# A two-layer decoder trunk (block-sparse attention, then gated DeltaNet): elementwise work moved from GpSimd to VectorE and ScalarE, and the order of all work planned anew

## The chip, the cores and the metric

The kernel runs on one core of a Trainium2 chip, in one launch. The metric is the device time of that launch in microseconds (us); the time before is 693.81 us, the median of three runs (692.59 to 696.28). A core has TensorE (PE; PEld is its weight load), VectorE (DVE), ScalarE (ACT), GpSimd (POOL) and SyncE (SP, which here only issues DMAs). Each works through its own list of instructions in order.

## The reference, cut to what matters

The input is x, 512 positions of 1024 values in float32, and a condition c. Two layers follow, each with weights of some 16 MB for its input projection:

```
for i in range(2):
    mod = silu(c) @ ada_w[i] + ada_b[i];  shift, scale, gate = split(mod, 3)
    h = x * (1 + scale) + shift
    y = moba_branch(h) if i == 0 else gdn_branch(h)
    x = layer_norm(sqrt(2) * x + gate * y)

moba_branch: q, k, v, z = split(h @ w_in)        # 8 heads of 128
    o = softmax over own 256-block (causal) and selected past blocks
    return (o * silu(z)) @ w_out
gdn_branch:  q, k, v, z, a, b = split(h @ w_in)
    q, k, v = silu(causal conv of 4 taps);  q, k L2-normalised
    g = -exp(a_log) * softplus(a + dt_bias);  beta = sigmoid(b)
    per head, chunks: solve (I + tril(beta * k k^T * decay)) for u, w,
    then the recurrence over chunks, RMS norm, times silu(z), @ w_out
```

## The kernel before, in words

All large products are float32 work done in three passes on a shorter format: each operand is split into a high half (ScalarE copies it, `wh`, `hH`, `oH`) and a low half (the rest, `wl`, `hL`, `oL`, a subtraction), and TensorE adds high x high, low x high and high x low (`mm3`). So each of the weight pieces that are read (`raw`, 512 KB each, two buffers, `fetch` at L254) has four subtractions of 512 columns per group of 256 weight columns behind it (`cut`, L268): the first of each half-piece on VectorE, the second on GpSimd. A raw buffer is free again when its last subtraction is done.

Stages. (1) Front: for each of eight column blocks j, `first_mod` computes the modulation from 1 MB of `aw` on VectorE (`accj`, some six multiply-adds of 256 columns), `first_h` makes block j of h (`hH`, `hL`), `first_w` splits a 768-column weight block (`wrh` on ScalarE, `wrl` on GpSimd except for j = 0), and `first_mm` multiplies into `z_ps`. (2) Layer 0: the other projections, attention (`att`, scores `s_ps`, probabilities `pr`, small statistics `nm`), and beside it the remaining modulations (`mods`, tile `acc`, from `ga`). The output projection (`out0`, `y_ps`) reads `wl_0o`, `wh_0o`; before these are cut, `cut` multiplies the raw weights by the layer's gate on GpSimd (`gate=0`). (3) Switch: `evac` adds the product to xn, `norm0` normalises, `mod_t` transposes to `h_ps` and makes the next `hH`, `hL`; `prep` loads small tensors (`crow`, `wab`, `dtb`) and transposes `crow` (`crow_t`); `residual` multiplies xn by `g0r` and adds `b0r` on GpSimd; `decays` computes the log decays (`spl`, `g_`, `gc`) in some 30 dependent small steps. (4) Layer 1: projections `gq`, `gk`, `gv`, `z`, convolutions (`conv`, `pre`), and for each of four pairs of heads `inverse` (triangular factor `L`, its block diagonal `Lc` through DRAM to `Lr`, 15 steps on `u`, then small 32-wide products `X_ps`, `U_ps`), `values` (transposes `vt_ps`), `recur`, `gated` (`ogn`, `og_ps`) and the output products `y_ps`. The other banks' results of layer 1 go through ScalarE (`et`) and are added on GpSimd (`evac1`). (5) Tail: `finish` normalises four row tiles (`fin`) and stores them.

What sets the order. The program is written by a planner at build time (`Weave`, L34 to L138): every piece of work is a generator that yields an engine and an assumed cost; the planner takes the piece that could start first, and among equals the one with the smaller number in `RANK` (L179). So all instruction lists, SP's DMAs too, are fixed by these numbers and costs. Engines marked DVE2 and POOL exclude one another in the planner's account. Line 148 is the helper through which every instruction is recorded, so in the profile all rows have that line and one goes by tiles.

Of the kernel before, what the change touches and what calls it, by code (L numbers as in the profile page):

```python
# [19 lines left out]
H = 8  # L20
# [10 lines left out]
def flat(ap, dims, offset=0):  # L31
    return bass.AP(tensor=ap.tensor, offset=ap.offset + offset, ap=dims)


class Weave:
# [78 lines left out]

    def run(self, *until):
        while True:
            self._settle()
            if all(u in self.marks for u in until):
                return
            best, first = None, None  # L120
            for p in self.pieces:
                if p[3][0] in ("slot", "wait"):
                    continue
                start = self._start(p[3][0], p[3][2])
                if best is None or start < first - 1e-6:
# [9 lines left out]
            self._go(best, first + cost + self.LAT.get(engine, 0.0))  # L135
# [29 lines left out]

@with_exitstack
def trunk(ctx: ExitStack, tc: tile.TileContext, x, c, ada_w, ada_b, ln_g, ln_b, moba_w_in, moba_w_out,
# [11 lines left out]
    RANK = dict(fetch=16, kv0=26, qk0=82, kv00=105, cols2=77, mods=48, loads=9, evac0=82, conv0=93, decays=4, evac1=82, zs=11, conv=65, prep=68, resid=21, decay_f=38, inverse=0, inner=102, queries=5, values=94, recur=87, gated=42, keep0=47, norm0=18, mod_t=85, cut0=63, cut1=78)  # L179
# [59 lines left out]
    for name, n in (("mm", 0), ("s", 0), ("t", 1), ("o", 0), ("raw", 2), ("wp", 2), ("wx", 2), ("aw", 3), ("wr", 3),  # L239
# [3 lines left out]
        pl.slots(name, n)  # L243
# [24 lines left out]
    def cut(g0, g1):  # L268
# [3 lines left out]
        for name, w, c0, slot, width, r0, nk, gate in groups[g0:g1]:  # L272
# [8 lines left out]
            for h in range(2):  # L281
                t = yield "wait", ("raw", name, h)
                t = max(t, t0)
                raw = raws.pop((name, h))
                if gate is not None:
                    t = max(t, (yield "wait", ("gate", gate)))
                    hk = nk // 2
                    r3 = raw.rearrange("p (k n) -> p k n", n=width)
                    t = yield "POOL", pool(1024), t
                    ge.tensor_mul(r3, r3, gates[gate][:, None, c0:c0 + width].to_broadcast([P, hk, width]))  # L290
                ends = []
                for q in range(2):
                    sl = slice(q * 512, q * 512 + 512)
                    r = raw[:, sl]
                    if wide == width:
                        d = slice(1024 * h + q * 512, 1024 * h + q * 512 + 512)
                        dh, dl = wh[:, d], wl[:, d]
                    else:
                        r = r.rearrange("p (k n) -> p k n", n=width)
                        d = slice(4 * h + 2 * q, 4 * h + 2 * q + 2)  # L300
                        dh, dl = wh3[:, d, 0:width], wl3[:, d, 0:width]
                    e = yield "ACT", act(512), t
                    se.activation(dh, r, AF.Copy)
                    eng = "POOL" if q and gate is None else "DVE"
                    e = yield (eng if eng == "POOL" else "DVE2"), (pool if eng == "POOL" else dve)(512), e
# [149 lines left out]
    def first_w(j):  # L455
# [12 lines left out]
        e = yield ("POOL", pool(768), e) if j else ("DVE2", dve(768), e)  # L468
        (ge if j else ve).tensor_sub(wl, wr, wh.bitcast(F32))
# [127 lines left out]
    def att(hd, i):  # L597
# [22 lines left out]
        else:  # L620
# [198 lines left out]
    def mod_t(hf, k2):  # L819
# [87 lines left out]
    def prep():  # L907
# [32 lines left out]

        yield "POOL", 0.8, 0.0
        low = l1.tile([P, 32], F32, name="low")
        ge.memset(low, 0.0)
        ge.memset(low[:, 0:16], 1.0)
        for g in range(4):
            lg = low[32 * g:32 * g + 32]
            ge.affine_select(lg, lg, pattern=[[0, 32]], compare_op=ALU.is_ge, fill=0.0, base=-16,
                             channel_multiplier=1)
# [9 lines left out]
        masks.update(blk=blk, low=low, blk32=blk32, id32=id32, d16=d16)  # L958
        pl.mark("masks", e)

    def residual():
# [6 lines left out]
        t = yield "wait", "out0", ("gate_row", 1)  # L968
# [8 lines left out]
        for st in range(ST):  # L977
            e = yield "wait", ("hT", st // 2, 0), ("hT", st // 2, 1), ("hT", st // 2, 2), ("hT", st // 2, 3)
            e = max(e, eg)
            for q in range(2):  # L980
                qs = slice(q * 512, q * 512 + 512)
                e = yield "POOL", pool(512), e
                ge.tensor_mul(xn[:, st, qs], xn[:, st, qs], g0r[:, qs])
                e = yield "POOL", pool(512), e
                ge.tensor_add(xn[:, st, qs], xn[:, st, qs], b0r[:, qs])
# [166 lines left out]
    def proj1():  # L1152
# [34 lines left out]
        for sp_ in order1[2:]:  # L1187
            s, p = sp_[0], int(sp_[1])
            dep = yield "wait", ("w", "1" + sp_)
            if s == "o":  # L1190
                for p_, st in last if p == H // 2 - 2 else [] if p == H // 2 - 1 else [(p, st) for st in range(ST)]:
# [4 lines left out]
                    for q in pq:  # L1196
                        if q == p_:
                            dep = max(dep, (yield "wait", ("ogT", p_, st)))
                        for g2 in range(2):
# [7 lines left out]
                            if q == p_:  # L1207
                                pl.add(RANK["evac1"], evac1(os_[g2], st, g2, f"y{p_}", e))
# [76 lines left out]
    def inverse(p):  # L1285
# [36 lines left out]
        for h in range(2):  # L1322
# [12 lines left out]
        fac[p, "L"] = L
        pl.mark(("L", p), e1)

        e = yield "POOL", pool(1024), e1
        Lm = f4(p, "Lm", tag="UT")
        ge.tensor_mul(v8(Lm), v8(L), masks["blk"][:, None, :].to_broadcast([P, 8, P]))  # L1340
        e = yield "DVE", 1.87, e
        Lc = f4(p, "Lc", [P, 8, 16])
        ve.reduce_sum(Lc, v8(Lm).rearrange("p t (b j) -> p t j b", j=16), axis=AX.X)
# [31 lines left out]
        e = yield "wait", ("Lb", p), ("aq", p)  # L1375
        Lb = fac[p, "Lb"]
# [3 lines left out]
        L8, U8 = v8(L), v8(Uf)  # L1380
# [3 lines left out]
        g32 = [slice(32 * g, 32 * g + 32) for g in range(4)]  # L1384
# [80 lines left out]

    def inner(p):

        e = yield "wait", ("L", p)
        Lb = fac[p, "Lb"] = f4(p, "Lb", [P, 8, 32])

        e += 2.5
        for g in range(4):
            pp = slice(32 * g, 32 * g + 32)
            e1 = yield "POOL", pool(256), e
            ge.tensor_mul(Lb[pp], v8(fac[p, "L"])[pp, :, pp], masks["low"][pp, None, :].to_broadcast([32, 8, 32]))
        pl.mark(("Lb", p), e1)
# [198 lines left out]
    def finish(st):  # L1675
# [26 lines left out]
        def normed(qs, e1, nb):  # L1702
# [4 lines left out]
            e1 = yield "POOL", pool(512), e1  # L1707
            ge.tensor_add(f[:, qs], f[:, qs], fin["b"][:, qs])
# [59 lines left out]
```

## Time and profile before

| | before |
|---|---|
| median of three runs | 693.81 us |
| profiled execution | 695.99 us, its span 694.3 us |
| busy: PE, DVE, ACT, POOL | 628.1, 507.6, 310.2, 246.1 us |
| mean granted clock of TensorE | 0.963 |
| read from HBM | 78.82 MB |

In the views a row of a timeline says: start, duration, engine, line, operation, tiles out<-in, shapes, count, and in brackets how long the engine was idle before it and what released it. Several equal instructions in a row are merged, the duration is then that of all. The last 0.08 us or so of a VectorE instruction overlap with the next one, so that two of 0.68 us take 1.28 us. PEclk is the clock that TensorE was granted: 1.00 is 2.4 GHz, 0.50 is 1.2 GHz.

### The profile page before, as it was taken

The page shows a single profiled execution, that of the slowest core. Times are in us where ns is not written, and L with a number is a line of the kernel's source. Part 1 is how long each engine was busy: PE and PEld are TensorE (multiplying, and loading weights), DVE is VectorE, ACT ScalarE, POOL GpSimd, SP SyncE. Part 2 cuts the span into 40 slices and gives each one's busy share as a digit, 9 for nine tenths or more (in the row PEclk, how much of TensorE's full clock was granted, in tenths as well). Part 3 has the DMA queues.
Part 4 walks back from the last instruction along what each step waited for, and adds up shares of the span by engine and source line. Part 5 has one row for each costly group of instructions (what it writes and reads, how often), then busy time and mean ns, then how long its engine had stood idle before and what let it go on. Part 6 is the DMA issues. An engine that isn't in the chain of part 4 may idle for free. (4 is left out here: it accounts for less than half of the span.)

```text
span 694.3 us, 12082 instructions
## 1 busy us (share of the span) xinstructions
PE 628.1 (90%) x4488; PEld 539.7 (78%) x4488; DVE 507.6 (73%) x1155; ACT 310.2 (45%) x822; POOL 246.1 (35%) x203
## 2 busy tenths in 40 slices
PE   8699999999999999599978979999999978999991
PEld 7588788977988778599866857788887757997871
DVE  5875888687685777367677678587737798688687
ACT  2334555543531334114334763765375457633451
POOL 0235122402214042305862352252226332744625
PEclk8899999999999999899999999999989989999997
DMA  9992645747545331504114353424133204412203
GB/s 262 298 290 78 187 137 176 242 143 224 152 156 168 102 122 62 159 2 122 31 34 90 92 141 85 117 58 133 33 91 84 77 2 117 135 59 64 92 2 121
DMA packets 83022, 82.25 MB, mean 118 GB/s; under 512 B 8762, under 2 KB 71443, under 8 KB 82451
## 3 DMA queue, kind: packets, MB, share of 16 engines
q1 hardware_dynamic: 82882, 81.45, 40.6%
q8 instruction: 35, 0.57, 0.3%
q14 instruction: 25, 0.20, 0.1%
q10 hardware_dynamic: 80, 0.03, 0.0%
HBM read 78.82 MB, written 2.65 MB: 117 GB/s over the span
## 5 line engine op out<-in xcount | busy, mean ns | idle before, releaser
L148 DVE SCALAR_TENSOR_TENSOR acc<-ga,cs,acc 128x512 f32<-128x512 f32 x56 | 51.1, 924 | 19.1 <-DMA ga<-in_ada_w_dram 19.0
L148 POOL TENSOR_TENSOR raw_0o<-raw_0o,gate 128x1024 f32<-128x1024 f32 x8 | 19.1, 2388 | 58.2 <-DMA raw_0o<-in_moba_w_out_dram 40.4
L148 ACT ACTIVATE pr<-s_ps,nm 128x256 f32<-128x256 f32 (+1 forms) x48 | 20.7, 436 | 41.0 <-DVE nm L148 35.6
L148 PE MATMUL z_ps<-wh_1z,hH 128*128 128x256 f32 (+1 forms) x128 | 37.8, 295 | 0.0
L148 PE MATMUL y_ps<-wh_0o,oH 128*128 128x256 f32 x128 | 37.7, 294 | 0.0
L148 PE MATMUL y_ps<-wh_0o,oL 128*128 128x256 f32 x128 | 37.0, 289 | 0.0
L148 PE MATMUL y_ps<-wl_0o,oH 128*128 128x256 f32 x128 | 37.0, 289 | 0.0
L148 PE MATMUL z_ps<-wh_1z,hL 128*128 128x256 f32 (+1 forms) x128 | 36.4, 285 | 0.0
L148 PE MATMUL z_ps<-wl_1z,hH 128*128 128x256 f32 (+1 forms) x128 | 36.4, 284 | 0.0
L148 PE MATMUL gk_ps<-hH,wl_1k 128*128 128x512 f32 x64 | 26.5, 415 | 3.6 <-DVE wl_1k L148 3.6
L148 POOL TENSOR_TENSOR wrl<-wr,wrh 128x768 fp32r<-128x768 f32 x7 | 14.0, 2002 | 44.6 <-ACT wrh L148 44.6
L148 PE MATMUL gq_ps<-hH,wh_1q 128*128 128x512 f32 (+1 forms) x80 | 29.5, 368 | 0.0
L148 PE MATMUL v_ps<-wh_0v,hH 128*128 128x256 f32 x96 | 28.3, 295 | 0.0
L148 PE MATMUL gq_ps<-hL,wh_1q 128*128 128x512 f32 (+1 forms) x80 | 27.9, 349 | 0.0
L148 PE MATMUL gk_ps<-hH,wh_1k 128*128 128x512 f32 x64 | 27.9, 435 | 0.0
L148 PE MATMUL gq_ps<-hH,wl_1q 128*128 128x512 f32 (+1 forms) x80 | 27.8, 348 | 0.0
L148 PE MATMUL gv_ps<-hH,wh_1v 128*128 128x512 f32 x64 | 27.8, 434 | 0.0
L148 PE MATMUL y_ps<-wh_1o,ogh 128*128 128x512 f32 x64 | 27.7, 432 | 0.0
L148 PE MATMUL z_ps<-hH,wh_0z 128*128 128x512 f32 x64 | 26.6, 416 | 1.0 <-ACT qT L148 1.0
L148 PE MATMUL v_ps<-wl_0v,hH 128*128 128x256 f32 x96 | 27.1, 283 | 0.0
L148 PE MATMUL v_ps<-wh_0v,hL 128*128 128x256 f32 x96 | 27.1, 283 | 0.0
L148 DVE SCALAR_TENSOR_TENSOR accj<-aw,cs,accj 128x256 f32<-128x256 f32 x45 | 26.4, 653 | 0.8 <-DMA aw<-in_ada_w_dram 0.8
(335 smaller groups left out, 2234.6 us busy)
## 6 DMA issues: line engine op xcount, KB each, us to landing
ga<-in_ada_w_dram SPq DMA_DIRECT2D x64, 256.0 KB
aw<-in_ada_w_dram SPq DMA_DIRECT2D x14, 512.0 KB
raw_0z<-in_moba_w_in_dram SPq DMA_DIRECT2D x8, 512.0 KB
raw_0o<-in_moba_w_out_dram SPq DMA_DIRECT2D x8, 512.0 KB
raw_1z<-in_gdn_w_in_dram SPq DMA_DIRECT2D x8, 512.0 KB
raw_1q<-in_gdn_w_in_dram SPq DMA_DIRECT2D x8, 512.0 KB
raw_1k<-in_gdn_w_in_dram SPq DMA_DIRECT2D x8, 512.0 KB
raw_1v<-in_gdn_w_in_dram SPq DMA_DIRECT2D x8, 512.0 KB
```

The source lines that it names most:

```text
L148: r = f(*args, **kwargs)
```

## The change

The planner can now leave an elementwise operation to either VectorE or GpSimd (`either`, `_choose`); it takes the one that would end first, with 49/20 = 2.45 us added for GpSimd. Of the operations that are offered so, all but two come out on VectorE. GpSimd's list shrinks from 183 rows to 60; what is left are the powers (`rstd`, `rk`, `rq`, `rms`), masks, memsets and two copies of `T64` per pair. Further: layer 0's gate no longer multiplies the weights but the product, in PSUM, on VectorE (12 tiles of 512 columns); the softmax's probabilities are scaled on ScalarE, and the small statistics that added or compared two tiles use a per-partition operand instead; `L` is made by four ScalarE scalings and one VectorE product for each head; `Lc` and `Lb` are taken with 32 small ScalarE and 16 VectorE instructions for the four pairs in place of GpSimd's masked products and VectorE's reduction; layer 1's results are all added by VectorE from PSUM (`evac1` is gone); z2 and z3 are projected earlier. All numbers in `RANK` are new. Cut to its core:

```diff
-    RANK = dict(fetch=16, ..., prep=68, resid=21, ..., mod_t=85, cut0=63, cut1=78)
+RANK = dict(pool=49, fetch=22, ..., prep=8, resid=0, ..., mod_t=58, cut0=75, cut1=78)
...
+    def _choose(self, engine, cost, dep):
+        if "/" not in engine:
+            return engine, cost, self._start(engine, dep)
+        ends = []
+        for n, c in zip(engine.split("/"), cost):
+            t = self._start(n, dep)
+            ends.append((t + c + (RANK["pool"] / 20 if n == "POOL" else 0.0), n, c, t))
+        return min(ends)[1:]
+def either(n, ptr=0):
+    return "DVE2/POOL", (dve(n, ptr), pool(n))
...
 cut
-                    t = yield "POOL", pool(1024), t
-                    ge.tensor_mul(r3, r3, gates[gate][...])
+                    t, g = yield *either(1024), t
+                    eng_(g).tensor_mul(r3, r3, gates[gate][...])
-                    eng = "POOL" if q and gate is None else "DVE"
-                    (ge if eng == "POOL" else ve).tensor_sub(dl, r, dh.bitcast(F32))
+                    e, g = yield *either(512), e
+                    eng_(g).tensor_sub(dl, r, dh.bitcast(F32))
...
-        want(f"0o{g}", moba_w_out[0], g * GW, "wx" if g < 2 else "wp", gate=0)
-    order1 = "z0 q0 k0 q1 v0 v1 k1 v2 q2 k2 z1 k3 q3 v3 o0 z2 z3 o1 o2 o3".split()
+        want(f"0o{g}", moba_w_out[0], g * GW, "wx" if g < 2 else "wp")
+    order1 = "z0 q0 k0 q1 v0 v1 k1 v2 q2 k2 z1 k3 q3 z2 v3 z3 o0 o1 o2 o3".split()
...
 first_w (mod_t, residual and finish alike)
-        (ge if j else ve).tensor_sub(wl, wr, wh.bitcast(F32))
+        e, g = yield *either(768), e
+        eng_(g).tensor_sub(wl, wr, wh.bitcast(F32))
...
 att
-            ve.tensor_max(m, m, nb)
+            ve.tensor_scalar(m, m, nb, None, op0=ALU.max)
-        ve.tensor_scalar_mul(pr[:, :n], pr[:, :n], rv)
+        se.activation(pr[:, :n], pr[:, :n], AF.Copy, scale=rv)
...
 evac
+        if first_ is not None:
+            e = max(e, (yield "wait", ("gate", 0)))
+            e = yield "DVE", dve(512), e
+            ve.tensor_mul(o, o, gates[0][:, gs])
...
 inverse
-                ve.scalar_tensor_tensor(L[:, h, t], gk[:, t], bk2[...], F[:, h, t], op0=ALU.mult, op1=ALU.mult)
+                se.activation(L[:, h, t], F[:, h, t], AF.Copy, scale=bk2[...])
+            ve.tensor_mul(L[:, h], gk, L[:, h])
-        ge.tensor_mul(v8(Lm), v8(L), masks["blk"][...])
-        ve.reduce_sum(Lc, v8(Lm).rearrange("p t (b j) -> p t j b", j=16), axis=AX.X)
+        for g in g32:
+            se.activation(Lc[g], L8[g, :, g.start:g.start + 16], AF.Copy, scale=half[0][g])
+        for g in g32:
+            ve.scalar_tensor_tensor(Lc[g], L8[g, :, g.start + 16:g.stop], half[1][g], Lc[g], ...)
```

Three places in the instruction lists. The first is SP's list of DMAs at the switch from layer 0 to layer 1, before:

```order
L148 DMA raw_0o_2661<-in_moba_w_out_dram 128x4x256
L148 DMA raw_0o_2763<-in_moba_w_out_dram 128x4x256
L148 DMA g0r<-in_ln_g_dram 128x1024
L148 DMA b0r<-in_ln_b_dram 128x1024
L148 DMA raw_0o_2860<-in_moba_w_out_dram 128x4x256
L148 DMA crow<-in_gdn_conv_w_dram 96x128
L148 DMA wab<-in_gdn_w_in_dram 128x8x16
L148 DMA dtb<-in_gdn_dt_bias_dram 128x8
L148 DMA dtb<-in_gdn_a_log_dram 128x8
L148 DMA raw_1z_2879<-in_gdn_w_in_dram 128x4x256
```

and after the change:

```order
L164 DMA raw_0o_2643<-in_moba_w_out_dram 128x4x256
L164 DMA raw_0o_2665<-in_moba_w_out_dram 128x4x256
L164 DMA raw_1z_2784<-in_gdn_w_in_dram 128x4x256
L164 DMA raw_1z_2805<-in_gdn_w_in_dram 128x4x256
L164 DMA g0r<-in_ln_g_dram 128x1024
L164 DMA b0r<-in_ln_b_dram 128x1024
L164 DMA crow<-in_gdn_conv_w_dram 96x128
L164 DMA wab<-in_gdn_w_in_dram 128x8x16
L164 DMA dtb<-in_gdn_dt_bias_dram 128x8
```

Here `raw_0o` are the weight pieces of layer 0's output projection, `raw_1z` the first of layer 1. The last `raw_0o` stood behind `g0r` and `b0r`, which need memory of the attention stage; now all `raw_0o` and the first `raw_1z` stand ahead of them.

The second is VectorE's list in the front, block j = 1 to j = 2, before:

```order
L148 SCALAR_TENSOR_TENSOR accj<-aw,cs,accj 128x256 x6
L148 TENSOR_TENSOR accj<-accj 128x256
L148 TENSOR_TENSOR hL<-ht,hH 128x512
L148 TENSOR_TENSOR ab_268<-mod_ps,colb 128x2
L148 TENSOR_SCALAR accj<-aw,cs 128x256 x2
L148 SCALAR_TENSOR_TENSOR accj<-aw,cs,accj 128x256 x6
L148 TENSOR_TENSOR accj<-accj 128x256
```

and after:

```order
L164 SCALAR_TENSOR_TENSOR accj<-aw,cs,accj 128x256 x6
L164 TENSOR_TENSOR accj<-accj 128x256
L164 TENSOR_TENSOR hL<-ht,hH 128x512
L164 TENSOR_TENSOR wrl<-wr,wrh 128x768
L164 TENSOR_TENSOR ab_273<-mod_ps,colb 128x2
L164 TENSOR_SCALAR accj<-aw,cs 128x256 x2
L164 SCALAR_TENSOR_TENSOR accj<-aw,cs,accj 128x256 x6
L164 TENSOR_TENSOR accj<-accj 128x256
```

One `wrl` subtraction of 768 columns per block has come into the list, behind the `hL` of the same block.

The third is TensorE's list in layer 1 where the values of the first pair of heads are transposed (`vt_ps`), before:

```order
L148 MATMUL gv_ps_1_3974<-hH,wh_1v_3763 128x512
L148 MATMUL gv_ps_1_3974<-hH,wl_1v_3764 128x512
L148 MATMUL gv_ps_1_3974<-hL,wh_1v_3763 128x512
L148 MATMUL vt_ps_0_4070<-ident,vc_4039 128x128 x4
L148 MATMUL gv_ps_0_4069<-hH,wh_1v_3887 128x512
L148 MATMUL gv_ps_0_4069<-hH,wl_1v_3888 128x512
L148 MATMUL gv_ps_0_4069<-hL,wh_1v_3887 128x512
L148 MATMUL vt_ps_1_4087<-ident,vc_4058 128x128 x4
L148 MATMUL gv_ps_0_4069<-hH,wh_1v_3887 128x512
```

and after:

```order
L164 MATMUL gv_ps_0_4060<-hH,wh_1v_3887 128x512
L164 MATMUL gv_ps_0_4060<-hH,wl_1v_3888 128x512
L164 MATMUL gv_ps_0_4060<-hL,wh_1v_3887 128x512
L164 MATMUL vt_ps_0_4108<-ident,vc_4042 128x128 x4
L164 MATMUL gv_ps_1_4105<-hH,wh_1v_3887 128x512
L164 MATMUL gv_ps_1_4105<-hH,wl_1v_3888 128x512
L164 MATMUL gv_ps_1_4105<-hL,wh_1v_3887 128x512
```

The transposes of `vt_ps_0` stood right behind the projection `gv_ps_1` of their own pair; now the 24 matmuls of the next pair's `gv_ps_0` stand between them, and nine more before `vt_ps_1`.

## Rows read from the trace of the kernel before

**Rows 1.** Page, parts 1 and 2: busy time of each engine; TensorE in 40 slices.

```profile
PE 628.1 (90%) x4488; PEld 539.7 (78%) x4488; DVE 507.6 (73%) x1155; ACT 310.2 (45%) x822; POOL 246.1 (35%) x203
...
PEclk8899999999999999899999999999989989999997
```

**Rows 2.** Waits of TensorE: for what; us in total, times, longest us.

```profile
PE crow_t L148 <- DMA wab<-in_gdn_w_in_dram: 7.5, 1, 7.5
PE mod_ps L148 <- DVE accj L148: 6.3, 3, 3.1
PE vt_ps L148 <- DVE vc L148: 4.5, 2, 3.8
PE gk_ps L148 <- DVE wl_1k L148: 3.6, 1, 3.6
...
PE pt_ps L148 <- DVE nm L148: 1.9, 2, 1.7
PE gate_ps L148 <- DVE mod L148: 1.7, 1, 1.7
PE h_ps L148 <- ACT ht L148: 1.6, 1, 1.6
```

**Rows 3.** Timeline at the switch: SP.

```profile
280.28 0.42 SPq L148 DMA_DIRECT2D raw_0o<-in_moba_w_out_dram  x1
280.75 0.50 SPq L148 DMA_DIRECT2D crow<-in_gdn_conv_w_dram  x1
```

**Rows 4.** The same stretch: GpSimd.

```profile
256.64 2.36 POOL L148 TENSOR_TENSOR raw_0o<-raw_0o,gate 128x1024 f32<-128x1024 f32 x1 [0.55 <-DMA raw_0o<-in_moba_w_out_dram]
...
287.05 2.36 POOL L148 TENSOR_TENSOR raw_0o<-raw_0o,gate 128x1024 f32<-128x1024 f32 x1 [9.81 <-DMA dtb<-in_gdn_dt_bias_dram]
```

**Rows 5.** The same stretch: TensorE.

```profile
287.35 0.39 PE L148 MATMUL crow_t<-ident,crow 96*128 96x96 f32 x1 [7.47 <-DMA wab<-in_gdn_w_in_dram]
```

**Rows 6.** The same stretch: VectorE.

```profile
248.63 1.28 DVE L148 TENSOR_TENSOR wl_0o<-raw_0o,wh_0o 128x512 fp32r<-128x512 f32 x2
...
256.66 2.36 DVE L148 TENSOR_TENSOR mod<-mod,colb 128x8 f32<-128x8 f32 x1
...
290.10 1.40 DVE L148 TENSOR_TENSOR wl_0o<-raw_0o,wh_0o 128x512 fp32r<-128x512 f32 x2 [9.31 <-ACT wh_0o L148]
```

**Rows 7.** Windows: us, busy by engine (count), PEclk, DMA share, GB/s.

```profile
35.00:40.00 5.00, 5.00 (x30) 4.31 (x29) 0.98 (x4) 1.53 (x2) 1.85 (x1) 0.93 1.15 305
...
285.00:290.00 5.00, 2.65 (x13) 2.68 (x14) 0.00 (x0) 0.56 (x2) 2.88 (x4) 0.50 0.62 162
...
295.00:300.00 5.00, 5.00 (x44) 5.00 (x44) 2.38 (x4) 0.00 (x0) 0.00 (x0) 1.00 0.01 3
...
290.00:680.00 390.00, 361.84 (x2949) 311.83 (x2948) 287.96 (x642) 194.94 (x560) 165.41 (x146) 0.97 0.28 76
680.00:694.00 14.00, 0.31 (x2) 0.00 (x0) 10.88 (x14) 1.52 (x2) 7.20 (x6) 0.65 0.35 134
```

**Rows 8.** Timeline, front, j = 1 to 4.

```profile
18.92 4.01 DVE L148 SCALAR_TENSOR_TENSOR accj<-aw,cs,accj 128x256 f32<-128x256 f32 x6
...
19.74 2.12 POOL L148 TENSOR_TENSOR wrl<-wr,wrh 128x768 fp32r<-128x768 f32 x1 [18.38 <-ACT wrh L148]
...
30.89 2.46 DVE L148 SCALAR_TENSOR_TENSOR accj<-aw,cs,accj 128x256 f32<-128x256 f32 x6
```

**Rows 9.** Groups by tile and shape: busy us, mean ns, idle before, releaser.

```profile
L148 DVE TENSOR_REDUCE Lc<-Lm 128x128 f32<-128x1024 f32 x4 | 7.8, 1939 | 1.3 <-POOL Lm L148 1.3
...
L148 DVE TENSOR_TENSOR xn<-xn,y_ps 128x512 f32<-128x512 f32 x23 | 15.7, 682 | 9.4 <-PE y_ps L148 9.0
```

**Rows 10.** Timeline in layer 1, first pair of heads: TensorE.

```profile
406.41 0.63 PE L148 MATMUL vt_ps<-ident,vc 128*128 128x128 f32 x4 [3.79 <-DVE vc L148]
```

**Rows 11.** Timeline of the tail: VectorE.

```profile
686.22 1.75 DVE L148 SCALAR_TENSOR_TENSOR fin<-xn,lnmv,g1r 128x512 f32<-128x512 f32 x1
```

**Rows 12.** Timeline of the tail: GpSimd.

```profile
684.41 4.68 POOL L148 TENSOR_TENSOR fin<-fin,b1r 128x512 f32<-128x512 f32 x3
```

More of the change, by code (lines that the diff above doesn't have):

```diff
@@ L32, in flat @@
     return bass.AP(tensor=ap.tensor, offset=ap.offset + offset, ap=dims)
+RANK = dict(pool=49, fetch=22, kv0=50, qk0=45, kv00=40, cols2=20, mods=50, loads=25, evac0=96, conv0=17, decays=11, evac1=60, zs=49, conv=45, prep=8, resid=0, decay_f=67, inverse=4, inner=0, queries=40, values=94, recur=96, gated=7, keep0=43, norm0=37, mod_t=58, cut0=75, cut1=78)
 class Weave:
@@ L119, in run @@
                 return
-            best, first = None, None
+            best, first, choice = None, None, None
             for p in self.pieces:
@@ L134, in run @@
             self.busy[engine] = first + cost
-            self._go(best, first + cost + self.LAT.get(engine, 0.0))
+            end = first + cost + self.LAT.get(engine, 0.0)
+            self.ran = engine, first, cost
+            self._go(best, (end, engine) if either else end)
 class InOrder:
@@ L177, in trunk, with eng_ @@
     DLAT = 2.0
-    RANK = dict(fetch=16, kv0=26, qk0=82, kv00=105, cols2=77, mods=48, loads=9, evac0=82, conv0=93, decays=4, evac1=82, zs=11, conv=65, prep=68, resid=21, decay_f=38, inverse=0, inner=102, queries=5, values=94, recur=87, gated=42, keep0=47, norm0=18, mod_t=85, cut0=63, cut1=78)
+    def eng_(name):
+        return ge if name == "POOL" else ve
     def dma(kb, dep=0.0):
@@ L939, in prep @@
                          channel_multiplier=-1)
[L941 to L948, printed above, removed]
         e = yield "DVE", 0.6, pl.busy["POOL"] + 0.2
@@ L967, in residual @@
         eg = e + DLAT
-        t = yield "wait", "out0", ("gate_row", 1)
+        t = yield "wait", "out0", ("gate_row", 1), *(("ya", st, q) for st in (2, 3) for q in range(2))
         e = yield dma(512, t)
@@ L981, in residual @@
                 qs = slice(q * 512, q * 512 + 512)
[L982 to L985, printed above, removed]
+                e, g = yield *either(512), e
+                eng_(g).tensor_mul(xn[:, st, qs], xn[:, st, qs], g0r[:, qs])
+                e, g = yield *either(512), e
+                eng_(g).tensor_add(xn[:, st, qs], xn[:, st, qs], b0r[:, qs])
         pl.mark("x1", e)
@@ L1327, in inverse @@
                 te.matmul(gk[:, t], kc[h][:, ts(t)], kc[h][:, ts(t)], start=True, stop=True)
-            e1 = max(e, e1, (yield "wait", ("F", p)), lev)
+            e2 = max(e, (yield "wait", ("F", p)), lev)
             F = fac[p, "F"]
             for t in range(ST):
-                e1 = yield "DVE", dve(128, 1), e1 - 0.2
-                ve.scalar_tensor_tensor(L[:, h, t], gk[:, t], bk2[:, t, h:h + 1], F[:, h, t], op0=ALU.mult,
-                                        op1=ALU.mult)
+                e2 = yield "ACT", act(128, 1), e2 - 0.2 * (t > 0)
+                se.activation(L[:, h, t], F[:, h, t], AF.Copy, scale=bk2[:, t, h:h + 1])
+            e1 = yield "DVE", dve(512), max(e1, e2)
+            ve.tensor_mul(L[:, h], gk, L[:, h])
             pl.give("s", e1)
[L1335 to L1341, printed above, removed]
-        Lc = f4(p, "Lc", [P, 8, 16])
-        ve.reduce_sum(Lc, v8(Lm).rearrange("p t (b j) -> p t j b", j=16), axis=AX.X)
+        Lc = f4(p, "Lc", [P, 8, 16])
+        Lb = f4(p, "Lb", [P, 8, 32])
+        yield "POOL", 0.3, 0.0
+        ge.memset(Lb, 0.0)
+        L8 = v8(L)
+        g32 = [slice(32 * g, 32 * g + 32) for g in range(4)]
+        half = [masks["blk32"][:, 0:1], masks["blk32"][:, 16:17]]
+        e2 = e1
+        for g in g32:
+            e2 = yield "ACT", act(128, 1), e2 - 0.2
+            se.activation(Lc[g], L8[g, :, g.start:g.start + 16], AF.Copy, scale=half[0][g])
+        e = e1 + 0.4
+        for g in g32:
+            e = yield "DVE2", dve(128, 1), e - 0.1
+            ve.scalar_tensor_tensor(Lc[g], L8[g, :, g.start + 16:g.stop], half[1][g], Lc[g], op0=ALU.mult, op1=ALU.add)
+        e = max(e, e2 + 0.4)
+        for g in g32:
+            e2 = yield "ACT", act(128, 1), e2 - 0.2
+            se.activation(Lb[g, :, 0:16], L8[g, :, g.start:g.start + 16], AF.Copy, scale=half[1][g])
         e = yield dma(128, e)
@@ L1379, in inverse @@
         fac[p, "Uf"] = Uf
[L1380 removed]
+        U8 = v8(Uf)
         yield "POOL", 1.1, 0.0
@@ L1464, in inverse @@
         pl.mark(("inv", p), e)
[L1466 to L1476, printed above, removed]
     def queries(p):
```

58 lines of the change are left out of this document (19 added, 39 removed), and 1 row of the table rcol.

## The prediction, made before the changed kernel was run

> **What bounds the kernel now.** I read the page first. TensorE is busy for 628.1 us of a span of 694.3, VectorE for 507.6 and GpSimd for 246.1 [rows 1]. TensorE executes the same set of matmuls before and after the change, in another order. So the change can win at most what TensorE loses: 66 us of idle time, 14 of them in the tail behind the last matmuls [rows 7], and what the stretches with a lower clock cost. The view of TensorE's waits, read next, says for whom it waits. The reader is to see there that the largest sum is one single wait of 7.5 us for `crow_t`, put down to a DMA (`wab`), and that most others end on VectorE: `mod_ps` 6.3, `vt_ps` 4.5, `gk_ps` 3.6, `pt_ps` 1.9, `gate_ps` 1.7 [rows 2]. So VectorE is waited for, without being full. Timelines of single stretches say why.
>
> At the switch no slow DMA is the cause. SP issued the last `raw_0o` only at 280.28, and `crow` behind it at 280.75 [rows 3]. GpSimd's product of that piece with the gate ran from 287.05 for 2.36 us [rows 4], and TensorE came back at 287.35 with `crow_t`, which stands next in its list [rows 5]; VectorE had idled for 9.31 us before its subtractions on `wl_0o` at 290.10 [rows 6]. Everything hangs on two late loads. The idle time has a second price: from 285 to 290 the granted clock is 0.50 (1.2 GHz) and 13 matmuls take 2.65 us, 0.204 each; from 295 to 300 it is 1.00 (2.4 GHz) and 44 take 5.00, 0.114 each [rows 7].
>
> Elsewhere it is GpSimd that slows VectorE. Six multiply-adds of `accj` take 4.01 us where `wrl` runs beside them on GpSimd, and 2.46 where nothing does [rows 8]. A `mod` of 8 columns on VectorE takes 2.36 us from 256.66 [rows 6], which is just GpSimd's gate product, 2.36 us from 256.64 [rows 4].
>
> **The change part by part,** against the profiled execution's own 695.99 us, which is 2.2 us above the median of 693.81. An undisturbed 512-column operation on VectorE takes (1.28 − 0.08)/2 = 0.60 us [rows 6]; other widths between SBUF tiles are estimated from it in proportion.
>
> VectorE's account, from the counts in the lists. In: 56 subtractions `wl` (33.6 us), seven `wrl` of 768 columns (6.3), 16 operations of the residual (9.6), eight `raw_1o` products of 1024 columns (9.6), 11 additions and 12 gate products with an operand in PSUM (23 × 0.68 = 15.6 [rows 9]), six for `fin` (3.6), 16 small ones for `Lc` (some 3): 81 us. Out: 32 scalings of probabilities (estimate 10), four reductions of 1.94 (7.8 [rows 9]), some 4 for `L`: 22. That is 59 us more. Against it stands the slowing, which goes: at the ratio of `accj` it is 4.01/2.46 − 1 = 0.63 us per us beside GpSimd, at most 246 × 0.63 = 155 us and at least 0. I take half, 77, since half or so of VectorE's instructions lie beside idle GpSimd or read PSUM. VectorE then stays at some 490 us. Its sum does not matter; that it no longer stalls just where TensorE waits does.
> The Trainium skill has a rule on this (SBUF — State Buffer, Who interferes with whom): VectorE and GpSimd share a port pair under an exclusive lock, and only instructions that need it contend. By it operations on PSUM win nothing from an idle GpSimd. The trace agrees: additions of `y_ps` have a mean of 0.682 us with GpSimd running [rows 9]. Without the rule the relief could be the 155, and the time that of rival C; by it, that of the forecast.
>
> (a) Front: −3 us. The `mod_ps` waits are 6.3 us [rows 2]. Six `accj` lose 4.01 − 2.46 = 1.55 us to GpSimd, and each block gets one `wrl` of 0.9 into VectorE's list. DMA at 305 GB/s from 35 to 40 [rows 7] sets the pace of the front, so I take half of the waits. Bounds: −6 (all) and −1.
>
> (b) Switch: −8.5 us. All `raw_0o` are now issued before `g0r` and `b0r`, and no gate product is between them and the subtractions, so the 7.5 us go. Late next is `crow`, which still waits for attention's memory: it needs 6.6 us from issue to use (280.75 to 287.35), and an estimated 4 to 5 before the issue, 11 in all. TensorE now has 138 matmuls of the output projection in between, 138 × 0.114 = 16 us. Of the low clock, 20 matmuls at 0.204 in place of 0.114 are 1.8 us; I count 1.0. Bounds: −9.3 and −3 (if eight gate products of 0.68 hold up the normalisation).
>
> (c) Small statistics in attention: −3 us. `gate_ps` and `pt_ps` wait 1.7 and 1.9 us [rows 2] for small instructions stalled by GpSimd. What may stand ahead of these now is a `wl` subtraction of 0.6 in the same list. Bounds: −3.6 and 0.
>
> (d) Start of layer 1: −1 us. The waits of `h_ps` (1.6) and `gk_ps` (3.6 [rows 2]) go, −5.2; of the 9.6 us of residual that come into the list of the decays, `wl_1k` and the first convolutions, I put 4.2 on the path. Bounds: −9 (their low clock too) and +6 (all 9.6, less 3.6).
>
> (e) `vt_ps`: −4 us. TensorE waited 3.79 us at 406.41 [rows 10] with independent matmuls behind. Now 24 of 512 columns stand ahead, 24 × 2 × 0.114 = 5.5 us. Bounds: −6 (with the low clock behind it) and 0 (if VectorE's `vc` comes later by as much).
>
> (f) Rest of layer 1: +4 us. From 290 to 680 VectorE is busy 288.0 of 390 us and TensorE 361.8 [rows 7]. Some 47 of the 81 us come in here, 11 of the 22 go out, and half of GpSimd's 165.4 times 0.63 is 52 of relief: VectorE's sum falls a little, but it is denser in the convolutions and `inverse`, and the matmuls that now cover `vt_ps` no longer stand between the small 32-wide products. One clock drop as at the switch (1.8 us) in two of four pairs is 3.6. Bounds: −6 (a third of the 18 us of idle time left there) and +14 (in each pair a drop and a wait like that of `gate_ps`, 4 × 3.5).
>
> (g) Tail: −1.3 us. GpSimd's three additions take 4.68 us [rows 12], three on VectorE 1.8: −2.9. A `fin` on VectorE that took 1.75 beside them [rows 11] gets shorter, but all stand in one list now; I give 1.6 back. Bounds: −2.9 and +1.
>
> Sum: −3 − 8.5 − 3 − 1 − 4 + 4 − 1.3 = −16.8. 695.99 − 16.8 = 679.2, less 2.2 is 677 for the median.
>
> **The rivals.** (A) VectorE becomes the bound behind the switch, from the last attention tile to layer 1's first convolutions, where evacuation, gate products, residual, decays and the `wl` of the first projections are one list. My count of that list gives 61 to 69 us against 68 to 73 us of matmuls; it decides once VectorE's work exceeds TensorE's. Price: 47 us move in; if a third ends on the path, +15.7, with only the gains of switch and tail kept (−9.8): 693.8 + 15.7 − 9.8 = 700; with half, 707. For it: VectorE's waits lead already. Against: it is idle for 102 us of 390 there, and loses the stalls.
> The Trainium skill speaks for it (Perfetto Trace Analysis, Optimizing Scalar/DVE Operations): a saturated VectorE should hand work to ScalarE or even GpSimd, and shifting work between VectorE and GpSimd might not help, as they share a port. By this the time would be A's; the 102 idle us say that VectorE is not saturated yet.
>
> (B) Only switch and tail gain, and the rest comes back as waits at the next place: 693.8 − 9.8 = 684. For it: VectorE's sum hardly changes. Against: TensorE waits directly for the stalled instructions.
>
> (C) Stalled VectorE was behind most idle time: of 66 us, 14 stay in the tail, two thirds of the other 52 go: 693.8 − 35 = 659. For it: nearly all waits of [rows 2] end on VectorE. Against: several hang on loads or on the order.
>
> (D) The stall at the switch only moves: `raw_1z` now stands ahead of `crow` on SP and waits for buffers that the last `raw_0o` subtractions free. Then (b) is 0, and with (f) at +10 the rest sums to −2: 692.
>
> **How the numbers follow.** Forecast 0.59 (own range 664 to 688), A 0.11, B 0.20, C 0.06, D 0.04. Differences under 0.5%, 3.5 us, can't be told from no change. Faster: forecast, B and C, 0.85, less 0.01 for the forecast's upper edge: 0.84. Same: D and that edge, 0.05. Slower: A, 0.11. The range 660 to 694 leaves out A, most of C and little else.
>
> **What would show it.** (a) `accj` at 2.5 us per six, `mod_ps` waits near 3. (b) No wait of `crow_t` over 1 us, and a clock of 1.00 through the switch. (c) No `mod` or `nm` over 0.5 us. (d) No wait of TensorE over 2 us before the first convolutions. (e) `vt_ps` without a wait. (f) VectorE at 470 to 520 us busy. (g) Under 13 us from the last matmul to the end. VectorE over 540 us, or a wait of over 3 us on a `wl` or a convolution, is A. The forecast is wrong if TensorE's idle time stays over 58 us or falls under 35.

## The result and the profile after

The changed kernel takes 674.29 us (median of 4 runs, 671.39 to 675.41) against 695.04 us before (4 runs beside it); the ratio is 0.9695, with a 95% interval of 0.9645 to 0.9744. A later run of the same kernel gave 0.9676 (0.9642 to 0.9710). The forecast was 677 us. The profiled execution took 675.41 us, its span is 673.7.

The page, parts 1 and 2, of the changed kernel; they answer to [rows 1]:

```profile
PE 626.9 (93%) x4488; PEld 541.7 (80%) x4488; DVE 500.9 (74%) x1229; ACT 339.3 (50%) x907; POOL 47.8 (7%) x67
...
PEclk8799999989999999999999999989789999999797
```

TensorE has the same matmuls and is busy for nearly the same time; of the 20.6 us less of span 19.4 are its idle time, which went from 66.2 to 46.8. GpSimd went from 246.1 to 47.8 us, and VectorE, which took over its work, is busy for 500.9 us against 507.6: the work that came in is about as large as the slowing that went.

TensorE's waits in the changed kernel, as in [rows 2]:

```profile
PE xt_ps L164 <- DMA xn<-in_x_dram: 4.2, 3, 2.2
PE os_ps L164 <- ACT y L164: 3.6, 5, 1.9
PE o_ps L164 <- ACT pt L164: 2.6, 2, 1.9
PE gk_ps L164 <- DVE wl_1k L164: 2.3, 1, 2.3
PE gk_ps L164 <- DVE L L164: 2.1, 1, 2.1
PE mod_ps L164 <- DVE accj L164: 1.8, 2, 1.2
PE og_ps L164 <- DVE ogn L164: 1.7, 2, 0.9
...
PE pt_ps L164 <- ACT pr L164: 1.3, 3, 0.6
...
PE h_ps L164 <- ACT ht L164: 0.6, 1, 0.6
```

`crow_t`, `vt_ps`, `gate_ps` and `pt_ps` on `nm` are gone from the list; `mod_ps` fell from 6.3 to 1.8 us, `gk_ps` on `wl_1k` from 3.6 to 2.3. At the top are now loads of x (`xt_ps`, 0.8 before) and short chains over ScalarE (`os_ps`, 2.1 before; `o_ps`, which is new).

By stage, in windows (us, then busy time and instructions of PE, PEld, DVE, ACT, POOL, granted clock, DMA share, GB/s): front; attention, up to its last `o_ps`; switch, up to the last matmul of layer 0; up to the first `vt_ps`; up to TensorE's last matmul; tail. Before:

```profile
0.00:66.10 66.10, 55.76 (x305) 49.31 (x305) 45.78 (x97) 20.85 (x31) 18.10 (x15) 0.90 0.86 232
66.10:275.20 209.10, 202.87 (x1187) 171.40 (x1187) 157.41 (x396) 90.58 (x227) 50.50 (x34) 1.00 0.51 159
275.20:327.70 52.50, 44.90 (x359) 44.49 (x358) 30.58 (x51) 13.54 (x24) 16.74 (x22) 0.93 0.29 80
327.70:406.40 78.70, 66.81 (x403) 58.19 (x403) 57.77 (x110) 35.95 (x100) 42.84 (x34) 0.98 0.28 72
406.40:680.30 273.90, 257.76 (x2240) 216.31 (x2240) 205.43 (x491) 147.79 (x439) 111.04 (x95) 0.97 0.29 80
680.30:694.30 14.00, 0.01 (x1) 0.00 (x0) 10.58 (x14) 1.52 (x2) 6.90 (x6) 0.64 0.34 131
```

After:

```profile
0.00:62.50 62.50, 54.52 (x305) 48.31 (x305) 45.00 (x110) 23.15 (x34) 0.70 (x6) 0.92 0.97 257
62.50:271.90 209.40, 203.85 (x1178) 170.96 (x1178) 144.68 (x389) 104.26 (x259) 3.63 (x5) 0.99 0.49 158
271.90:316.20 44.30, 44.04 (x367) 43.62 (x366) 31.54 (x60) 9.39 (x19) 3.00 (x8) 1.00 0.24 74
316.20:394.80 78.60, 72.62 (x429) 63.08 (x428) 62.75 (x138) 44.67 (x122) 7.13 (x7) 0.98 0.36 90
394.80:659.40 264.60, 251.86 (x2217) 215.74 (x2215) 206.27 (x515) 156.31 (x473) 30.82 (x39) 0.95 0.28 79
659.40:673.70 14.30, 0.00 (x0) 0.00 (x0) 10.65 (x22) 1.57 (x3) 2.52 (x2) 0.69 0.34 129
```

So the front is 3.6 us shorter, attention 0.3 us longer, the switch 8.2 us shorter, layer 1 (fourth and fifth window) 9.4 us shorter, the tail 0.3 us longer: 20.6 in all. In the profile of the later run no stage differs from these by more than 1.1 us. In layer 1 TensorE is busy for 324.6 us before and 324.5 after.

At the switch, SP's list and then TensorE's `crow_t` and the clock (compare [rows 3, 5, 7]):

```profile
270.33 2.41 SPq L164 DMA_DIRECT2D raw_1z<-in_gdn_w_in_dram  x2
274.42 0.35 SPq L164 DMA_DIRECT2D g0r<-in_ln_g_dram  x1
...
275.29 0.42 SPq L164 DMA_DIRECT2D crow<-in_gdn_conv_w_dram  x1
```

```profile
288.30 0.25 PE L164 MATMUL crow_t<-ident,crow 96*128 96x96 f32 x1
```

```profile
285.00:290.00 5.00, 5.00 (x44) 5.00 (x44) 4.89 (x10) 0.00 (x0) 0.00 (x0) 1.00 0.00 0
```

The pieces of `raw_1z` are issued at 270.33, ahead of `g0r`; `crow` is issued 13 us before its transposition, which comes without a wait amid 44 matmuls at full clock.

In the front six `accj` take 2.46 us in each of the six blocks where they stand in one row (compare [rows 8]), and the first `vt_ps` starts without a wait ([rows 10]):

```profile
28.63 2.46 DVE L164 SCALAR_TENSOR_TENSOR accj<-aw,cs,accj 128x256 f32<-128x256 f32 x6
```

```profile
394.77 0.60 PE L164 MATMUL vt_ps<-ident,vc 128*128 128x128 f32 x4
```

### The profile page after: what moved, and what is told of

It is laid out like the page before. It is cut to its first block, busy times and chain, and to the rows that moved or that the text cites. A ratio compares the mean times of both kernels' runs of the same rounds, so it can differ in the third digit from the quotient of the medians.

```text
span 673.7 us, 11993 instructions
## 1 busy us (share of the span) xinstructions
PE 626.9 (93%) x4488; PEld 541.7 (80%) x4488; DVE 500.9 (74%) x1229; ACT 339.3 (50%) x907; POOL 47.8 (7%) x67
## 4 chain that ended last, share of the span: by engine, by line
PE 60%; DVE 15%; DMA 11%; ACT 7%; SPq 3%; issue 3%; POOLq 0%; POOL 0%; ACTq 0%; DVEq 0%
PE z_ps L164 12%; PE y_ps L164 10%; PE gk_ps L164 6%; DMA ga<-in_ada_w_dram 6%; PE gv_ps L164 6%; PE gq_ps L164 5%; SPq L164 3%; PE k_ps L164 3%; PE q_ps L164 3%; PE v_ps L164 3%; DVE nm L164 3%; PE os_ps L164 2%; DVE acc L164 2%; DMA FX<-gcd 2%; DVE xn L164 2%
## 5 line engine op out<-in xcount | busy, mean ns | idle before, releaser
L164 DVE SCALAR_TENSOR_TENSOR acc<-ga,cs,acc 128x512 f32<-128x512 f32 x56 | 41.3, 746 | 25.8 <-DMA ga<-in_ada_w_dram 25.6
L164 PE MATMUL z_ps<-wh_1z,hH 128*128 128x256 f32 (+1 forms) x128 | 39.7, 310 | 2.3 <-DVE pre L164 1.3
L164 PEld LDWEIGHTS z_ps<-wh_1z,hH 128*128 128x128 f32 x128 | 25.2, 197 | 3.3 <-ACT hH L164 1.3
L164 DVE TENSOR_SCALAR nm<-nm 128x1 f32<-128x1 f32 x128 | 23.4, 189 | 4.2 <-ACT pr L164 1.3
L164 DVE TENSOR_REDUCE nm<-s_ps 128x1 f32<-128x128 f32 (+1 forms) x64 | 21.8, 383 | 5.7 <-PE s_ps L164 5.5
```

Source lines behind the costliest of these rows:

```text
L164: r = f(*args, **kwargs)
```

## The experiments

Two theories stood at the start. The own one: there are two separate causes, GpSimd stalling VectorE by running (8 to 9 us) and the order of loads and matmuls (some 12 us). The rivals: one of the two makes the whole gain. Ratios are to the kernel before, in runs beside it on the same chip.

**1. Engines alone, in the lists of before.** The planner keeps its old costs, so no list is re-ordered; only the engine that executes is another.

```diff
-                    (ge if eng == "POOL" else ve).tensor_sub(dl, r, dh.bitcast(F32))
+                    ve.tensor_sub(dl, r, dh.bitcast(F32))
```

and likewise the gate products, `wrl`, the residual, the sums, the block masks and `fin`.

> The lists of the kernel before with nothing re-planned, but every elementwise operation that GpSimd shared out of the weight splits, gates, residual, sums and block masks is emitted on VectorE instead. Own theory (two causes: stalls of VectorE beside GpSimd, worth some 8 to 9 us, and the order of loads and matmuls, worth some 12): about 685 us, 682 to 689, with the wait of crow_t still at 5 us or more and the wait of vt_ps still there. Rival 1 (the stalls alone made the gain): 680 or less. Rival 2 (the order alone made it): 692 or more.

Measured 685.69 us, ratio 0.9840 (0.9812 to 0.9868): as the own theory said. Busy times and waits:

```profile
PE 627.3 (92%) x4488; PEld 541.2 (79%) x4488; DVE 526.0 (77%) x1289; ACT 310.5 (46%) x822; POOL 52.5 (8%) x69
```

```profile
PE xt_ps L148 <- DMA xn<-in_x_dram: 6.3, 5, 2.2
PE crow_t L148 <- DMA dtb<-in_gdn_dt_bias_dram: 6.3, 1, 6.3
PE vt_ps L148 <- DVE vc L148: 5.2, 1, 5.2
...
PE mod_ps L148 <- DVE accj L148: 1.8, 2, 1.1
```

The engines alone give 1.6%, though VectorE is busy for 18 us more than before. The waits of `crow_t` and `vt_ps` stay: they were not GpSimd's. The waits on `accj` fell from 6.3 to 1.8 us, and loads of xn have taken their place. Over half of the gain lies in attention, where TensorE hardly waits any more:

```profile
66.00:268.40 202.40, 201.72 (x1186) 171.55 (x1187) 158.41 (x426) 89.51 (x226) 0.84 (x3) 1.00 0.52 162
```

The Trainium skill (Perfetto Trace Analysis, Optimizing Scalar/DVE Operations) says that moving work between GpSimd and VectorE might not help because they share a port. Here it helped, from GpSimd to VectorE: by 1.6% with the same lists.

**2. Engines undone, in the lists of after.** The reverse: `ge` for the second low half of each piece, `wrl`, `raw_1o`, the residual and six additions of `fin`.

```diff
-                    eng_(g).tensor_sub(dl, r, dh.bitcast(F32))
+                    (ge if q and gate is None else ve).tensor_sub(dl, r, dh.bitcast(F32))
```

> The lists of the changed kernel with nothing re-planned, but the second low half of each weight piece, wrl of seven blocks, the raw_1o products, the residual and six additions of fin are emitted on GpSimd again. Own theory (stalls worth 8 to 9 us, order 12): about 683 us, 680 to 687, VectorE busy about as now (some 500 us) though it does fewer operations, no wait of crow_t over 1 us. Rival 1 (the stalls made the whole gain): 690 or more. Rival 2 (the order made it): 677 or less.

Measured 699.79 us, ratio 1.0053 (1.0030 to 1.0077), slower than before. My numbers failed; by them it is rival 1. With experiment 1 there are four corners: in the lists of before 1.0000 (GpSimd) and 0.9840 (VectorE), in those of after 1.0053 and 0.9695. The two causes do not add. The engines are worth 1.6% in the old lists and 3.6% in the new, and the new lists gain nothing with this much work on GpSimd. Two limits: the lists of after also hold the rest of the change (softmax scaling, `L` and `Lc` on ScalarE, the gate in PSUM, no `evac1`), of which only the gate was tried by itself; and they were planned for VectorE, so how an order planned for GpSimd would do in the new code is not shown.

```profile
PE 635.6 (91%) x4488; PEld 545.0 (78%) x4488; DVE 492.7 (71%) x1128; ACT 339.3 (49%) x907; POOL 198.0 (28%) x168
```

```profile
PE pt_ps L164 <- ACT pr L164: 4.9, 5, 1.9
...
PE og_ps L164 <- DVE ogn L164: 4.6, 4, 1.6
PE mod_ps L164 <- DVE accj L164: 4.5, 2, 3.1
```

VectorE executes 101 instructions fewer than in the changed kernel and is busy only 8 us less. There is no wait of `crow_t`. The four corners by stage, in us of the profiled executions, cut at the same matmuls as the windows above:

| stage | old lists, GpSimd | old lists, VectorE | new lists, GpSimd | new lists, VectorE |
|---|---|---|---|---|
| front | 66.1 | 66.0 | 62.3 | 62.5 |
| attention | 209.1 | 202.4 | 220.6 | 209.4 |
| switch | 52.5 | 51.1 | 44.3 | 44.3 |
| layer 1 | 352.6 | 349.8 | 354.6 | 343.2 |
| tail | 14.0 | 12.9 | 15.1 | 14.3 |

The stages say more than the totals. The front and nearly all of the switch go with the lists, whatever the engine. Attention goes with the engine, and there the new lists lose 7 us or more, about what the engine gives. In layer 1 the new lists gain only with VectorE.

**3. GpSimd's presence alone.** The changed kernel, with three subtractions of 128 columns on a scratch tile behind each weight split (the second of each half-piece), `wrl` and residual addition.

```diff
+    def again(a):
+        for b in range(3):
+            ge.tensor_sub(scr, scr, a[:, b * 128:b * 128 + 128].bitcast(F32))
```

> The changed kernel with about 100 times three added GpSimd subtractions of 128 columns, on a scratch tile, each time after a weight split or a residual addition; nothing waits for them but the reuse of the tiles that they read, and the results are thrown away. Own theory (GpSimd's work stalls VectorE just by running): VectorE's busy time rises by 30 to 60 us at the same instructions, and the time by 5 to 10 us, to 679 to 685. Rival (GpSimd cost time only as a slow link in chains that wait for its results): 676 or less.

Measured 687.21 us, ratio 0.9881 (0.9848 to 0.9913): 1.9% or 13 us over the changed kernel, more than I expected, though VectorE's busy time grew by less than the 30 to 60 us that I had put.

```profile
PE 627.9 (92%) x4488; PEld 540.7 (79%) x4488; DVE 520.5 (76%) x1229; ACT 339.1 (50%) x907; POOL 210.6 (31%) x329
```

VectorE's list is unaltered, and it is busy for 19.6 us more. Nothing needs the results of the added work, but the powers, masks and copies of layer 1 queue behind it on GpSimd. In attention, where GpSimd has next to no other work, the loss is already 4 to 6 us (last `o_ps` at 277.6; at 271.9 and 273.7 in two profiles of the changed kernel). So running GpSimd is itself a cost, and the rival falls; how much of the loss in layer 1 is that queue was not separated.

**4. The same dose on VectorE.** `ve` in place of `ge` in the lines of experiment 3.

> The changed kernel with the same 100 times three added subtractions of 128 columns as in the run with more GpSimd work, here on VectorE; nothing waits for their results, and these are thrown away. Own theory (in these lists TensorE waits so often on VectorE that its time counts by the half): VectorE busy 550 to 570 us, time 697 to 714. Rival (VectorE has 170 us of slack, only stalls inside short chains cost): 687 or less.

Measured 705.62 us, ratio 1.0116 (1.0080 to 1.0153).

```profile
PE 635.8 (90%) x4488; PEld 544.6 (77%) x4488; DVE 567.2 (80%) x1491; ACT 339.2 (48%) x907; POOL 47.1 (7%) x67
```

66.3 us more of VectorE's time cost 0.0421 × 695 = 29 us: 0.44 us per us (0.38 to 0.51 by the intervals), at 74% busy. The rival, that 170 us of idle time are slack, falls. Hence rival A of the prediction was nearer than it looked: by this price, which holds for work put behind the weight splits, another 50 us on VectorE would leave nothing of the gain (an estimate).

**5. The old order of loads at the switch.**

```diff
                 t = yield "slot", "raw"
+                if name == "0o3" and h:
+                    yield "wait", "b0r"
                 t = yield dma(512, t)
```

with `b0r` marked once its load is issued. SP's list has `g0r` and `b0r` ahead of the last `raw_0o` and of `raw_1z` again; TensorE's list is all but unaltered.

> The changed kernel with SP's list at the switch as it was: g0r and b0r ahead of the last raw_0o piece and of raw_1z. Own theory (the two late loads behind the held-up g0r were the stall, not the gate product): TensorE stops again for 4 to 8 us before crow_t or a matmul on wl_0o, its clock falls to 0.50, and the time is 680 to 684. Rival (the product on GpSimd between load and split was the stall): within 2 us of the changed kernel, 672 to 676.

Measured 682.88 us, ratio 0.9802 (0.9765 to 0.9839): 1.07% or 7.4 us over the changed kernel; in the profiled spans it is 5.3. From the last `o_ps` to the end of layer 0 it takes 49.5 us, against 44.3 in the changed kernel and 52.5 before. SP, the waits, and the clock from 280 to 290:

```profile
277.55 0.35 SPq L164 DMA_DIRECT2D g0r<-in_ln_g_dram  x1
...
278.42 0.43 SPq L164 DMA_DIRECT2D raw_0o<-in_moba_w_out_dram  x1
```

```profile
PE y_ps L164 <- ACT wh_0o L164: 3.2, 1, 3.2
```

```profile
280.00:285.00 5.00, 2.83 (x24) 2.62 (x22) 0.00 (x0) 0.00 (x0) 0.00 (x0) 1.00 0.85 304
285.00:290.00 5.00, 3.72 (x20) 3.51 (x21) 3.89 (x6) 1.15 (x2) 0.00 (x0) 0.77 0.61 128
```

The last `raw_0o` leaves at 278.42, TensorE waits 3.2 us for `wh_0o` and its clock falls to 0.77 in the mean of the next window. Nothing ran on GpSimd here: a late load makes a stall without the gate product. It is shorter than the 7.5 us of before, where the product of 2.36 us stood between load and use; the product's share was not separated.

**6. The gate on the weights again,** on VectorE, without the products in PSUM.

```diff
-        want(f"0o{g}", moba_w_out[0], g * GW, "wx" if g < 2 else "wp")
+        want(f"0o{g}", moba_w_out[0], g * GW, "wx" if g < 2 else "wp", gate=0)
```

> The changed kernel with layer 0's gate on the weights again (eight products of 1024 columns, on VectorE, ahead of the splits) and no products in PSUM; the order is planned anew by the same numbers. Own theory (where the gate stands matters little once the loads are early): 672 to 679. Rival (the product between load and split held up the weights at the switch): 680 or more, with a wait of 2 us or more on wh_0o or wl_0o.

Measured 686.14 us, ratio 0.9839 (0.9796 to 0.9882). The planner left seven of the eight products to VectorE and one to GpSimd. The time is the rival's, its reason is not: there is no wait on `wh_0o` or `wl_0o`, and from the last `o_ps` to the end of layer 0 it takes 44.7 us, against 44.3 in the changed kernel (layer 0 ends at 318.8; at 316.2 and 318.0 in two profiles of the changed kernel). Nearly all of the loss comes in layer 1, where the planner, fed with other costs, chose another order:

```profile
PE z_ps L164 <- DVE ut L164: 4.2, 1, 4.2
```

```profile
559.00:573.00 14.00, 13.57 (x90) 10.99 (x91) 8.17 (x15) 5.87 (x13) 0.00 (x0) 0.51 0.53 144
```

14 us at 1.2 GHz where the changed kernel runs at 2.4; behind the first `vt_ps` it is 41 us at 1.2 GHz in all, against 24. About the gate this run says no more than that it cost some 0.4 us at its place.

**7. The old numbers in the new code.** Only RANK is that of before, with `pool=49`.

> The code of the changed kernel with the RANK numbers of the kernel before (pool stays 49). In its lists the loads at the switch already stand as after the change, raw_0o and raw_1z ahead of g0r, while vt_ps stands close behind its own projection as before. Own theory (engines and the loads come from the code, the numbers give only the order in layer 1): 677 to 684, no wait of crow_t over 1 us, a wait of vt_ps of 2 us or more. Rival 1 (the numbers are the order's whole share): 685 or more. Rival 2 (the numbers give nothing): 676 or less.

Measured 709.89 us, ratio 1.0185 (1.0145 to 1.0225): 34 us over the changed kernel, and slower than before; by the number it is rival 1. The own theory holds up to the end of layer 0 (318.3 us; 316.2 in the changed kernel, 327.7 before): engines and loads come from the code. In layer 1 it is far off. TensorE in the first pair's output, and three windows:

```profile
481.81 0.27 PE L164 MATMUL og_ps<-ident,ogn 128*128 128x128 f32 x1
487.19 0.85 PE L164 MATMUL og_ps<-ident,ogn 128*128 128x128 f32 x2 [5.12 <-DVE ogn L164]
488.37 1.09 PE L164 MATMUL kt_ps<-ident,kc 128*128 128x128 f32 x4 [0.33 <-DVE u L164]
```

```profile
486.00:514.00 28.00, 23.15 (x285) 19.35 (x285) 15.06 (x42) 15.85 (x51) 2.71 (x4) 0.51 0.34 96
514.00:561.00 47.00, 43.56 (x279) 38.27 (x277) 32.37 (x90) 31.88 (x106) 7.60 (x8) 1.00 0.22 60
561.00:582.00 21.00, 18.26 (x267) 16.73 (x268) 10.44 (x24) 6.58 (x14) 0.78 (x2) 0.51 0.33 88
```

From 481.81 to 504 no projection stands in TensorE's list among `og_ps`, `kt_ps` and the 32-wide products: TensorE waits 5.12 us on VectorE, and then stretches of 28 and 21 us run at a mean of 0.51. Why the planner leaves them out there was not traced further. The order of layer 1 can cost more than the whole change gains.

**8 to 10. Filling the gaps.** The changed kernel still has 13.6 us at 0.50 from 480. A run of the unaltered kernel went beside two with matmuls that are overwritten later:

```diff
         ups = pst("t", [P, 8, 32], f"U_ps{p}_32")
+        if p == 1:
+            fill(ups.rearrange("p a b -> p (a b)"), 8)
```

> The changed kernel once more, unaltered, as the measure for the two runs beside it: 672 to 676.

> The changed kernel with 46 matmuls whose results are overwritten, put where TensorE waits in layer 1 next to the small 32-wide products of the second and fourth pair and ahead of the first os_ps: nothing else is changed. Own theory (the idle gaps there bring the clock down to 0.50 for 13.6 us from 480 and 6.8 us from 623, and TensorE loses about half of that): the clock stays at 1.00 there, 668 to 671. Rival 1 (VectorE's chain bounds these stretches, so a faster TensorE only waits longer): 673 to 676 with the clock at 1.00. Rival 2 (the added matmuls delay the chain): 677 or more.

> The same, and in the front 10 such matmuls ahead of each of the two transposes (xt_ps) that wait for xn. Own theory (TensorE bounds the front from 30 us on, so half clock from 23 to 34 costs it some 3 us): the front's last matmul 2 to 4 us earlier than in the unaltered kernel, 665 to 669 in all. Rival (the front is bound by its loads): no change against the run without them in the front.

Measured 675.28 (0.9676, 0.9642 to 0.9710), 678.89 (0.9722, 0.9687 to 0.9758) and 677.29 us (0.9715, 0.9671 to 0.9759): no gain by either. The first is in rival 2's range, but the intervals overlap with that of the unaltered kernel, so a loss is not shown. The 4 us before the clock falls and the end of the stretch at half clock, first in the changed kernel, then in the one with the fillers:

```profile
476.40:480.40 4.00, 2.66 (x159) 2.04 (x160) 2.44 (x6) 2.13 (x4) 0.00 (x0) 1.00 0.02 4
486.00:494.00 8.00, 8.00 (x52) 7.54 (x52) 7.63 (x13) 4.75 (x10) 0.00 (x0) 0.50 0.27 79
```

```profile
475.70:479.70 4.00, 3.16 (x109) 2.65 (x109) 3.36 (x8) 2.50 (x5) 0.78 (x2) 1.00 0.01 4
486.00:493.00 7.00, 7.00 (x42) 6.54 (x42) 6.00 (x11) 3.84 (x9) 0.00 (x0) 0.50 0.40 111
```

The fillers raise TensorE's busy time before the fall from 2.66 to 3.16 us of 4.00, and the clock falls all the same, at 479.7 in place of 480.4, and stays at 0.50 for as long. My forecast of a clock of 1.00 failed. That does not clear the idle gaps: 0.84 us of them were left, and the largest filler, the eight matmuls shown above, began at 479.5. Whether the gaps that are left or the small products themselves bring the clock down was not shown. Gaps do not explain why it stays down: from 486 on TensorE has none in either kernel. In the front the ten added matmuls ahead of each of two `xt_ps` left its end at 62.5 us, against 62.3 with the other fillers alone, though it had 6.8 us at 0.50 in place of 10.2: the rival's forecast. No version beat the changed kernel.

## Why the prediction was right, point by point

- **VectorE's account** (490 us; measured 500.9): sound. With the 59 us that I counted in, 66 us of slowing went, where I had put 77; `accj` takes 2.46 us in each of the six blocks. The Trainium skill's rule (SBUF — State Buffer, Who interferes with whom), by which operations on PSUM win nothing, agrees: additions of `y_ps` have a mean of 0.683 us after and 0.682 before ([rows 9]). Of all 31 before, 11 lay beside work of GpSimd, with a mean of 0.686; the prediction wrote as if all did.
- **(a) front, −3:** measured −3.6 (−2.5 in the profile of the later run), but by another cause. In experiment 1 the `accj` are fast, `mod_ps` waits 1.8 us, and the front still ends at 66.0; in experiment 2 they are slow in two of the six blocks (4.0 us), `mod_ps` waits 4.5, and it ends at 62.3. So the gain is the new lists'; which row of them makes it I have not shown.
- **(b) switch, −8.5:** right in cause and in size, −8.2 from the last `o_ps` to the end of layer 0. Putting the old loads back brings 5.2 of that again, and `crow_t` no longer waits. What makes the other 3 us was not separated.
- **(c) statistics in attention, −3:** did not come; the stage took 209.1 us before and 209.4 after. The relief was there, and larger than I put it: in experiment 1 the stage takes 202.4, and TensorE idles in it for 0.7 us, against 6.2 before. In the changed kernel it idles for 5.6 again, for ScalarE: `o_ps` on `pt` 2.6, `z_ps` on `qT` 1.7, `pt_ps` on `pr` 1.3. I had not asked what the new lists and the work moved to ScalarE would take back; which of the two does it was not separated.
- **(d) start of layer 1, −1:** about −2. `h_ps`, `gk_ps` on `wl_1k`, `gc_ps` and `gct_ps` waited 8.1 us together, now 6.0 with the new waits on `hH` and `hL`. `gk_ps` still waits 2.3, above the 2 that I had set as a sign.
- **(e) `vt_ps`, −4:** right, −4.5, and by the order: the wait is 5.2 us in experiment 1 and absent in experiment 2.
- **(f) rest of layer 1, +4:** the term that was wrong, in its sign. Layer 1 gained 9.4 us; less (d) and (e) some −3 remain, within the bounds of −6 to +14. I had VectorE denser and two more drops of the clock. Behind the first `vt_ps` there are three stretches at 0.50 as before, but 24 us long in place of 17; still TensorE's busy time in layer 1 did not grow, and its idle time there fell from 28.0 to 18.7 us. With the old numbers the same code loses 34 us, nearly all in layer 1, so this stage could have gone far beyond the bounds. That this order was a good one could not be read from the profile of before.
- **(g) tail, −1.3:** measured +0.3. VectorE's busy time behind the last matmul is 10.65 us for 22 instructions against 10.58 for 14: the work that came in and the lost slowing cancel. With 14.3 us the sign of under 13 failed.

The sum was right to 4 us (−16.8 forecast, −20.6 in the spans) because (f) erred by 7 us one way and the others together by 3 the other; so far the closeness is luck. What was right by its mechanism is (b) and (e), and (d) in part; (a) came by another cause, (c) and (g) did not come. Of the rivals, A did not occur, though experiment 4 shows that its price is real; C and D are excluded by the time and by `crow_t`; B (684) was 10 us off, since layer 1 gained too.

## What to carry to other kernels

An engine at 74% busy can still set the time: find its price with a dose of added work (here about 0.44 us per us) before calling its idle time slack. When work changes engines under a planner, swap the engine with the lists kept, and the lists with the engine kept; the four corners here were 1.000, 0.984, 1.005 and 0.970, and no one of them shows the others. Read them by stage: a wait that is gone is not time won, as attention shows here, where new waits took its place. Look in the DMA queue for a load that stands behind one held by memory: it cost 5 to 7 us here, and the wait was put down to another load.

## What was not expected of the hardware

GpSimd work whose results nobody needs cost VectorE 19.6 us of busy time for 163 us of GpSimd's (210.6 against 47.8): 0.12 us per us, against 0.63 for six `accj` beside a `wrl`. TensorE's clock stayed at 0.50 for some 14 us from the small products on, in the last 8 of them without a gap in TensorE's work.
